# Transposes of the softmax weights moved from a step's middle to the next step's beginning, in a hybrid decoder layer

## The chip, the cores and the metric

The kernel runs on one core of a Trainium2 chip. The metric is the device time of one execution in microseconds (us). The engines are TensorE (PE; PEld is its weight load), VectorE (DVE), ScalarE (ACT), GpSimd (POOL) and SyncE (SP), which issues most DMAs. Each engine works through its own list of instructions in the order in which the program wrote them; semaphores tie the lists together.

## The reference

One decoder layer over 512 positions, width 2048, in float32. Cut to what matters:

```python
h = rmsnorm(x, g_pre_attn) * (1 + sc_a) + sh_a          # sc_a, sh_a: adaLN, silu(c) @ w_ada
qa, ka, va, qb, kb, vb = split(h @ w_in)                 # 8 heads A, 8 heads B, 128 wide
qa, ka, qb, kb = rope(...)
oa = rmsnorm(dilated_mixture_attention(qa, ka, va), g_out_a)     # group A: three dilated windows
s = einsum('bqmhe,bkmhe->bmhqk', qb, kb); a = softmax(causal(s)) # group B: two maps a head
ob = rmsnorm(einsum('bhqk,bkhe->bqhe', a[:,0] - lam * a[:,1], vb), g_subln) * (1 - lambda_init)
x = x + gt_a * rmsnorm(concat([oa, ob]) @ w_out, g_post_attn)
h = rmsnorm(x, g_pre_ffn) * (1 + sc_f) + sh_f
x = x + gt_f * rmsnorm((silu(h @ w_gate) * (h @ w_up)) @ w_down, g_post_ffn)
```

## The kernel before

The program is a list of 610 steps. Each step takes one weight tile of 128x1024 and multiplies it: steps 0 to 79 are the input projections, 80 to 143 the output projection (64 shorter steps), 144 onward the feed-forward part. Float32 accuracy comes from three products for each: a weight tile is split into a high part (w_hi, a ScalarE copy, L1710) and the rest (w_lo, a VectorE subtraction, L1719), and both meet the split activations. A step of the projections has 24 such products of 512 columns (L277 to L279, or L282 to L284), in two halves of 12. The split for step i + 2 is made during step i.

All other work is hung onto the steps by lists of functions. The loop over steps runs them in this order, and that sets every engine's order:

```
start_ev, pe_ev (by a number: 0, 1, 2), start2_ev, first half of the products, w_hi for i+2,
mid_ev, mid_act, second half of the products, post_ev, post_late + rope1, w_lo for i+2, rope2, dots, post_end
```

Attention runs in steps 20 to 79, beside the projections, as 56 units. A unit is one block of 128 queries of one head (for the first two blocks of a head of group A: both at once). A head of B has four units, a head of A three, and a planner places at most one unit in a step, in the order of the heads. A unit has these stages:

- s0, at a step's beginning: the scores on TensorE (L507 for B, L500 for A) into bank 4 or 5, on VectorE the mask with the row maximum (L512) and its negative (L515), on ScalarE the exponential (L516) into misc_p.
- s0b (post_late, B alone): VectorE joins the two maps (L521 to L524).
- s1, in the middle of the next step: one to four transposes of 128x128 on TensorE (L529) into bank 6. s1b: the ScalarE copy of them out of bank 6 (L534), into misc_pt, or into pts for the heads A4 to A7.
- s2, at the beginning of the step after: the products with V (L545) into bank 7. The heads A4 to A7 do theirs in steps 81 to 84.

After the last unit of a head its output is normalised: a, the ScalarE copy out of bank 7 (L558); b, four squares with row sums on ScalarE (L568), for B behind a VectorE maximum (L563 to L566); c, VectorE's small operations on the sums (L575 to L584) and a power on GpSimd (L585); c2, one step later, the scaling on VectorE (L589, L590); d, four transposes of the result (L595) into bank 6 as well, with the ScalarE copy L597 out of it.

In the same steps run the rotations of queries and keys: the evacuation of a finished projection (L413) and DMAs that swap rows, issued by ScalarE (L399), and one or two steps later three VectorE operations of 1024 columns (L426 to L428).

What fills the rest of VectorE are the dots: 96 products with row sums over tiles of w_ada (L228), for the adaLN values that are needed later. Each takes a tile of its own, loaded by SyncE (L1695) through the same four buffers as the weight tiles. The planner walks through the steps, adds up what TensorE, VectorE and the loads have to do (pe_cost, dve_cost and constants), and gives each step none, one or two dots, and each rotation its step, so that VectorE's sum stays near the end of TensorE's sum. Moving a cost from one step to another therefore shifts dots and rotations too. One group of 16 values is turned into a row by a transpose (L1018, with the copy L1020), two steps after its last dot, in the middle of a step and in bank 6.

In the output projection (steps 80 to 143) VectorE also splits the attention's result (L843) and scales finished sums (L1146).

Of the kernel before, what the change touches and what calls it, by code (L numbers as in the profile page):

```python
# [34 lines left out]
def body(tc, t):  # L35
# [5 lines left out]
    with ctx:  # L41
# [273 lines left out]
        pe_ev = defaultdict(list)  # L315
        mid_ev = defaultdict(list)
        post_ev = defaultdict(list)
# [284 lines left out]
        pe_cost = defaultdict(float)  # L602
        dve_cost = defaultdict(float)

        def place_unit(n, kind, head, qbs, hn, s):
            s0, s0b, s1, s1b, s2 = unit_stages(n, kind, head, qbs)
            m = 1 if kind == "A" else 2
            for qb in qbs:
                N = 128 * (qb + 1)
                pe_cost[s] += m * max(0.218, 0.00168 * N)  # L610
                dve_cost[s] += m * (0.4 + N / 960) + (1.0 + 1.6 * N / 960 if kind == "B" else 0)
                pe_cost[s + 1] += 0.107 * (qb + 1)
            if 0 in qbs:
                def mk(kind=kind, head=head):
                    h = HST[kind, head]
                    hs = sp.tile([128, 5, 4], F, name="hst", tag="hst", bufs=4)
                    for i, k in enumerate(("den", "ss", "f", "rd", "nb")):
                        h[k] = hs[:, i, :]
                pe_ev[s].append((0, mk))
            pe_ev[s].append((2, s0))  # L620
            post_late[s].append(s0b)
            mid_ev[s + 1].append(s1)
            mid_act[s + 1].append(s1b)
            if kind == "A" and head >= 4:
                late_pv[head].append(s2)
                assert s + 1 < W0
                return
            for qb in qbs:
                pe_cost[s + 2] += 0.218 * (qb + 1)
            pe_ev[s + 2].append((0, s2))  # L630
            if 3 in qbs:
                a, b, c, c2, d = head_post(kind, head, hn)
                start2_ev[s + 2].append(a)
                mid_act[s + 2].append(b)
                post_late[s + 2].append(c)
                post_ev[s + 3].append(c2)
                pe_ev[s + 4].append((1, d))
                dve_cost[s + 2] += 1.0 if kind == "A" else 1.6
                dve_cost[s + 3] += 0.8
                pe_cost[s + 4] += 0.43  # L640

        late_pv = defaultdict(list)

# [11 lines left out]
        post_late = defaultdict(list)  # L655
        rope1, rope2 = defaultdict(list), defaultdict(list)
        mid_act = defaultdict(list)
        dve_late = defaultdict(float)
        post_end = defaultdict(list)
        start2_ev = defaultdict(list)  # L660
# [204 lines left out]
        W0 = NPROJ  # L865
# [3 lines left out]
        for jj, kp in enumerate(KP_ORDER):  # L869
            for k in range(2):  # L870
                kc = 2 * kp + k
                s = wsteps[0, 0, jj, 0]
# [177 lines left out]
        for h in range(4, 8):  # L1050
            s = W0 + 1 + (h - 4)
# [4 lines left out]
        for i in range(W0 + 60):  # L1056
            mm_t = 5.13 if i < W0 else 2.57
            if todo:
                hn, k, h, qbs = todo[0]
                if need[k, h] == 0 and avail.get((k, h), -1) < i:  # L1060
                    todo.pop(0)
                    place_unit(nu, k, h, qbs, hn, i)
                    nu += 1
                    if not todo:
                        scored = i
# [199 lines left out]
        def act_tr(g, half, src, banks):  # L1265
            st = {}

            def go_pe():
                a = v3(src(), 2)
                for f in range(2):  # L1270
                    st[f] = ps = PS(banks[f], (128, 2, 256))
                    for n in range(2):
                        for tl_ in range(2):
                            c = 128 * (2 * n + f)
                            pe.transpose(ps[:, n, 128 * tl_:128 * tl_ + 128], a[:, tl_, c:c + 128], ident)  # L1275

            def go_v():
                stage.add(src())
                p = actv[g, f"v{half}"] = stage.get()
                for f in range(2):  # L1280
                    act.activation(v3(p, 4)[:, 2 * f:2 * f + 2, :], st[f], AF.Copy)
            return go_pe, go_v
# [105 lines left out]
        for hf, at in ((0, F0 + 32), (1, F0 + 36)):  # L1388
            a, b = act_tr(0, hf, lambda hf=hf: ffn["f0", hf], (6, 7))
# [10 lines left out]
        for g in range(1, 11):  # L1400
# [13 lines left out]
            a, b = act_tr(g, 0, lambda g=g: ffn[g, "s1"], (6, 7))  # L1414
            pe_ev[b0 + 27].append((0, a))
            post_ev[b0 + 27].append(b)
            a, b = act_tr(g, 1, lambda g=g: ffn[g, "c21"], (6, 7))
# [156 lines left out]
        for i in range(8):  # L1574
            a, b = h2_tr(0, i, 4 + i % 4)
# [16 lines left out]
        for i in range(8):  # L1592
            a, b = h2_tr(1, i, 4 + i % 4)
# [183 lines left out]
        for i in range(NSTEP):  # L1777
# [10 lines left out]
            s = steps[i]  # L1788
# [148 lines left out]
```

## Time and profile before

| | us |
|---|---|
| median of 3 runs (lowest, highest) | 2186.57 (2186.1, 2186.99) |
| the profiled execution | 2187.89 |
| its span, first to last instruction | 2186.1 |
| steps 20 to 79, from first to last | about 230 to 676 |

The profile shows one execution. Busy times of engines overlap. A row of time order reads: start, length, engine, line, operation, what it writes and reads, and in brackets the idle time of the engine before it and what ended that. A row of the waits reads: who waited for whom, total us, times, longest. A row of a group of instructions ends with its busy time and mean ns, and the idle time before them.

### The profile page before, as it was taken

What the parts mean: (1) busy time and instruction counts of PE and PEld (TensorE: products, weight loads), DVE (VectorE), ACT (ScalarE), POOL (GpSimd) and SP (SyncE); (2) the same over time, 40 slices, a digit from 0 to 9 for tenths busy, and PEclk for the clock granted to TensorE, in tenths of its full rate; (3) what the DMA queues carried; (4) which work ended last, traced back from release to release, by engine and by line L of the source; (5) the groups of instructions that cost most, each with busy time, mean ns of one, the idle gap of its engine ahead of it and who ended that gap; (6) DMA issues with size and microseconds to landing.
All of it is one profiled execution on the core that took longest, in us unless ns stands there. A gap on an engine that the chain in (4) does not pass through costs nothing.

```text
span 2186.1 us, 26913 instructions
## 1 busy us (share of the span) xinstructions
PE 2152.3 (98%) x9748; PEld 1758.3 (80%) x9748; DVE 1671.9 (76%) x2337; ACT 1058.1 (48%) x1541; POOL 103.7 (5%) x112
## 2 busy tenths in 40 slices
PE   7999999999999999999999999999999999999998
PEld 6888777778888788787888888888888888888886
DVE  6987877776777775896777777677777788898877
ACT  5443344444435565654545555554554553444443
POOL 0000000001001000000001001000000000000000
PEclk8999999999999999999999999999999999999999
DMA  9797634555678877787779769778777889999986
GB/s 374 298 347 227 170 113 155 168 157 173 208 239 275 285 248 262 264 291 220 219 228 271 224 207 289 214 202 267 241 223 221 279 310 410 381 386 369 345 304 264
DMA packets 160452, 564.39 MB, mean 258 GB/s; under 512 B 17440, under 2 KB 17728, under 8 KB 153920
## 3 DMA queue, kind: packets, MB, share of 16 engines
q1 hardware_dynamic: 142608, 502.09, 64.0%
q0 software_dynamic: 10944, 39.85, 10.2%
q10 hardware_dynamic: 6768, 20.73, 3.1%
q8 instruction: 77, 1.26, 0.2%
q14 instruction: 55, 0.45, 0.1%
HBM read 499.67 MB, written 54.02 MB: 253 GB/s over the span
## 4 chain that ended last, share of the span: by engine, by line
PE 88%; DMA 5%; DVE 4%; ACT 1%; issue 1%; SPq 0%; ACTq 0%; POOL 0%; DVEq 0%
PE b L283 22%; PE b L282 22%; PE b L284 22%; PE b L277 6%; PE b L279 5%; PE b L278 5%; PE b L507 2%; DMA w_raw<-in_wout 2%; DVE w_lo L1719 1%; DMA a<-acts 1%; PE b L545 1%; PE b L1275 1%; PE b L500 1%; PE b L529 1%; ACT w_hi L1710 1%
## 5 line engine op out<-in xcount | busy, mean ns | idle before, releaser
L1719 DVE TENSOR_TENSOR w_lo<-raw,w_hi 128x1024 fp32r<-128x1024 f32 x236 | 286.8, 1221 | 155.2 <-ACT w_hi L1710 155.1
L1710 ACT ACTIVATE w_hi<-raw 128x1024 fp32r<-128x1024 f32 x236 | 249.5, 1061 | 291.1 <-PE b L284 219.8
L282 PE MATMUL b<-w_hi,h 128*128 128x512 f32 x864 | 342.9, 397 | 0.4 <-ACT xT L212 0.4
L283 PE MATMUL b<-w_lo,h 128*128 128x512 f32 x864 | 337.0, 390 | 0.8 <-DVE w_lo L1719 0.7
L284 PE MATMUL b<-w_hi,h 128*128 128x512 f32 x864 | 336.9, 390 | 0.0
L1719 DVE TENSOR_TENSOR w_lo<-w_raw,w_hi 128x1024 fp32r<-128x1024 f32 x176 | 214.0, 1221 | 60.7 <-ACT w_hi L1710 60.5
L1710 ACT ACTIVATE w_hi<-w_raw 128x1024 fp32r<-128x1024 f32 x176 | 185.6, 1056 | 152.1 <-PE b L284 66.1
L282 PE MATMUL b<-w_hi,e 128*128 128x512 f32 x640 | 250.3, 391 | 4.1 <-ACT w_hi L1710 4.1
L283 PE MATMUL b<-w_lo,e 128*128 128x512 f32 x640 | 250.8, 392 | 1.0 <-DVE w_lo L1719 1.0
L284 PE MATMUL b<-w_hi,e 128*128 128x512 f32 x640 | 250.0, 391 | 0.0
L283 PE MATMUL b<-w_lo,a 128*128 128x512 f32 x616 | 240.0, 390 | 1.3 <-DVE w_lo L1719 1.3
L282 PE MATMUL b<-w_hi,a 128*128 128x512 f32 x616 | 240.0, 390 | 0.7 <-DMA a<-acts 0.7
L284 PE MATMUL b<-w_hi,a 128*128 128x512 f32 x616 | 239.7, 389 | 0.0
L1710 ACT ACTIVATE w_hi<-w_lent 128x1024 fp32r<-128x1024 f32 x130 | 137.8, 1061 | 172.8 <-PE b L284 130.3
L277 PE MATMUL b<-h,w_hi 128*128 128x512 f32 x512 | 213.4, 417 | 0.0
L278 PE MATMUL b<-h,w_hi 128*128 128x512 f32 x512 | 201.1, 393 | 1.4 <-DVE h L273 1.4
L279 PE MATMUL b<-h,w_lo 128*128 128x512 f32 x512 | 201.5, 394 | 0.0
L1719 DVE TENSOR_TENSOR w_lo<-w_lent,w_hi 128x1024 fp32r<-128x1024 f32 x130 | 158.5, 1220 | 56.0 <-ACT w_hi L1710 55.7
L282 PEld LDWEIGHTS b<-w_hi,h 128*128 128x128 f32 x864 | 162.3, 188 | 37.0 <-issue 3.8
L283 PEld LDWEIGHTS b<-w_lo,h 128*128 128x128 f32 x864 | 162.4, 188 | 35.3 <-DVE w_lo L1719 2.3
L284 PEld LDWEIGHTS b<-w_hi,h 128*128 128x128 f32 x864 | 162.2, 188 | 34.1
L516 ACT ACTIVATE misc_p<-misc_p,stt 128x128 f32<-128x128 f32 (+3 forms) x96 | 54.0, 562 | 190.2 <-DVE stt L515 171.5
(358 smaller groups left out, 3504.2 us busy)
## 6 DMA issues: line engine op xcount, KB each, us to landing
a<-acts SPq DMA_DIRECT2D x154, 512.0 KB, 5.7
raw<-in_wgu SPq DMA_DIRECT2D x131, 512.0 KB, 6.0
w_raw<-in_win SPq DMA_DIRECT2D x107, 512.0 KB, 4.9
w_raw<-in_adar SPq DMA_DIRECT2D x96, 512.0 KB, 4.6
w_lent<-in_wgu SPq DMA_DIRECT2D x69, 512.0 KB, 6.8
w_raw<-in_wout SPq DMA_DIRECT2D x64, 512.0 KB, 4.9
acts<-stage SPq DMA_DIRECT2D x49, 512.0 KB, 4.2
raw<-in_wds SPq DMA_DIRECT2D x48, 512.0 KB, 6.4
```

The source lines that it names most:

```text
L277: pe.matmul(ps, whi, ahi, start=start, stop=False, **kw)
L278: pe.matmul(ps, whi, alo, start=False, stop=False, **kw)
L279: pe.matmul(ps, wlo, ahi, start=False, stop=stop, **kw)
L282: pe.matmul(ps, ahi, whi, start=start, stop=False, **kw)
L283: pe.matmul(ps, ahi, wlo, start=False, stop=False, **kw)
L284: pe.matmul(ps, alo, whi, start=False, stop=stop, **kw)
L500: pe.matmul(sc[:, r], qk[:, i, qs], qk[:, i + 1, :N], start=True, stop=True)
L507: pe.matmul(sc[:, :N], qk[k, 2 * m, qs], qk[k, 2 * m + 1, :N], start=True, stop=True)
L516: act.activation(p, p, AF.Exp, bias=nm, scale=scale, accum_out=den)
L529: pe.transpose(tr[:, j, :], misc["p"][:, n % 2, 128 * j:128 * j + 128], ident)
L1710: act.activation(hi, raw, AF.Copy)
L1719: dve.tensor_tensor(lo, raw, hi.bitcast(F), op=OP.subtract)
```

## The change

Six entries of the function that places a unit change:

- s1 and s1b go from the middle of step s + 1 to step s + 2: the transposes to its beginning, behind the products with V of the unit before and ahead of the new scores; the copy behind the exponentials of that step and ahead of the weight split.
- s2 goes from step s + 2 to step s + 3, and a, b, c, c2 one step later with it.
- d goes from the beginning of step s + 4 to the middle of step s + 5.
- The planner's costs move to the same steps.

```diff
@@ place_unit
-                pe_cost[s + 1] += 0.107 * (qb + 1)
+                pe_cost[s + 2] += 0.107 * (qb + 1)
...
             pe_ev[s].append((2, s0))
             post_late[s].append(s0b)
-            mid_ev[s + 1].append(s1)
-            mid_act[s + 1].append(s1b)
+            pe_ev[s + 2].append((1, s1))
+            start2_ev[s + 2].append(s1b)
             if kind == "A" and head >= 4:
                 late_pv[head].append(s2)
-                assert s + 1 < W0
+                assert s + 2 < W0
                 return
             for qb in qbs:
-                pe_cost[s + 2] += 0.218 * (qb + 1)
-            pe_ev[s + 2].append((0, s2))
+                pe_cost[s + 3] += 0.218 * (qb + 1)
+            pe_ev[s + 3].append((0, s2))
             if 3 in qbs:
                 a, b, c, c2, d = head_post(kind, head, hn)
-                start2_ev[s + 2].append(a)
-                mid_act[s + 2].append(b)
-                post_late[s + 2].append(c)
-                post_ev[s + 3].append(c2)
-                pe_ev[s + 4].append((1, d))
-                dve_cost[s + 2] += 1.0 if kind == "A" else 1.6
-                dve_cost[s + 3] += 0.8
-                pe_cost[s + 4] += 0.43
+                start2_ev[s + 3].insert(0, a)
+                mid_act[s + 3].append(b)
+                post_late[s + 3].append(c)
+                post_ev[s + 4].append(c2)
+                mid_ev[s + 5].append(d)
+                dve_cost[s + 3] += 1.0 if kind == "A" else 1.6
+                dve_cost[s + 4] += 0.8
+                pe_cost[s + 5] += 0.43
```

The units keep their steps. The order of the instructions changes at these places, among others.

TensorE, step 64 before: the beginning of the step where the head A2 ends its work. First the end of step 63, then the step's own work, up to its first product; bank 7 is b_4450, bank 6 is b_4511.

```order
L279 MATMUL b_4283<-h_3_220,w_lo 128x512
L545 MATMUL b_4450<-VA_3018,misc_pt 128x128 [waits Activation_49]
L545 MATMUL b_4450<-VA_3018,misc_pt 128x128 x2
L595 MATMUL b_4511<-cst,misc_pt 128x128 [waits DVE_49,PE_49]
L595 MATMUL b_4511<-cst,misc_pt 128x128 x3
L500 MATMUL b_4518<-A_4267 128x128
L500 MATMUL b_4518<-A_4267 128x256
L277 MATMUL b_4527<-h_0_442,w_hi 128x512
```

TensorE, step 65 of the change, where the same head's L595 now stand: the last products of the first half, the transposes, the first products of the second half. Their bank 6 (b_4570) was written at this step's beginning by L529 (as b_4544).

```order
L277 MATMUL b_4501<-h_1_606,w_hi 128x512
L278 MATMUL b_4501<-h_1_616,w_hi 128x512
L279 MATMUL b_4501<-h_1_606,w_lo 128x512
L595 MATMUL b_4570<-cst,misc_pt 128x128 [waits DVE_49,Activation_49]
L595 MATMUL b_4570<-cst,misc_pt 128x128 x3
L277 MATMUL b_4502<-h_1_606,w_hi 128x512
L278 MATMUL b_4502<-h_1_616,w_hi 128x512
```

The transposes went from the beginning to the middle, and wait for ScalarE in place of an earlier instruction of TensorE.

ScalarE, steps 65 and 66 before (from the exponential of step 65), and then the same two steps of the change:

```order
L516 ACTIVATE misc_p,hst<-misc_p,stt 128x384 [waits DVE_49]
L558 ACTIVATE misc_pt<-b_4450 128x512 [waits PE_49]
L1710 ACTIVATE w_hi<-w_raw 128x1024 [waits DMAHW6_49]
L568 ACTIVATE junk,hst<-misc_pt 128x128 [waits Activation_49] x4
L534 ACTIVATE pts_4604<-b_4596 128x384 [waits PE_49]
L516 ACTIVATE misc_p,hst<-misc_p,stt 128x512 [waits DVE_49]
```

```order
L516 ACTIVATE misc_p,hst<-misc_p,stt 128x384 [waits DVE_49,PE_49]
L534 ACTIVATE misc_pt<-b_4544 128x512 [waits PE_49]
L1710 ACTIVATE w_hi<-w_raw 128x1024 [waits DMAHW1_49]
L597 ACTIVATE mixT_4212<-b_4570,cst 128x512 [waits PE_49]
L516 ACTIVATE misc_p,hst<-misc_p,stt 128x512 [waits DVE_49,PE_49,Activation_49]
L558 ACTIVATE misc_pt<-b_4481 128x512
L534 ACTIVATE pts_4613<-b_4602 128x384
```

The copy L534 went from the step's end to right behind the exponential, ahead of the weight split L1710 (and, where a head ends, ahead of the squares L568, which follow that split); L558 comes a step later, and L597 stands in the middle.

VectorE, steps 96 to 99 of the change in the output projection:

```order
L843 TENSOR_TENSOR mixlo_5798<-mixT_2288,mixhi_5797 128x256 x2
L1719 TENSOR_TENSOR w_lo<-w_raw,w_hi 128x1024
L228 SCALAR_TENSOR_TENSOR w_raw,red<-w_raw,p_82 128x1024
L1146 TENSOR_TENSOR u_5791<-b_5307,gtg_5203 128x512
L1146 TENSOR_TENSOR u_5793<-b_5314,gtg_5203 128x512
L1719 TENSOR_TENSOR w_lo<-w_raw,w_hi 128x1024
L228 SCALAR_TENSOR_TENSOR w_raw,red<-w_raw,silu_b 128x1024
L843 TENSOR_TENSOR mixlo_5798<-mixT_2288,mixhi_5797 128x256 x2
L1146 TENSOR_TENSOR u_5791<-b_5346,gtg_5203 128x512
L1146 TENSOR_TENSOR u_5793<-b_5357,gtg_5203 128x512
L1719 TENSOR_TENSOR w_lo<-w_raw,w_hi 128x1024 x2
L228 SCALAR_TENSOR_TENSOR w_raw,red<-w_raw,p_82 128x1024
```

Before, no L228 stood there: the last one was in step 94. Four dots more than before lie behind step 80: in steps 96, 97, 99 and 100, each with its load. Among the projections' steps some dots change places, the rotations of the heads B6, B7, A0 and A1 stand one step earlier (steps 29, 33, 45 and 49), and the row transpose L1018 goes from the middle of step 49 to the middle of step 54.

## The prediction

> **What bounds the kernel now.** I read the page's first part and its chain of waits, then the table of waits of TensorE, then the busy time by stretches, and last the engines in order of time around the attention work.
>
> ```profile
> PE 2152.3 (98%) x9748; PEld 1758.3 (80%) x9748; DVE 1671.9 (76%) x2337; ACT 1058.1 (48%) x1541; POOL 103.7 (5%) x112
> PE 88%; DMA 5%; DVE 4%; ACT 1%; issue 1%; SPq 0%; ACTq 0%; POOL 0%; DVEq 0%
> ...
> PE b L283 <- DVE w_lo L1719: 4.8, 9, 0.7
> PE b L529 <- ACT tabs L1020: 0.4, 1, 0.4
> ...
> 313.80:482.00 168.20, 167.84 (x771) 128.23 (x770) 129.12 (x343) 76.60 (x189) 5.03 (x5) 1.00 0.49 151
> 482.00:571.80 89.80, 89.80 (x454) 73.53 (x453) 62.28 (x134) 40.78 (x101) 7.39 (x4) 1.00 0.60 194
> 579.50:675.80 96.30, 96.30 (x441) 77.46 (x440) 68.19 (x128) 37.84 (x78) 1.82 (x1) 1.00 0.75 237
> 727.60:736.70 9.10, 8.47 (x37) 6.63 (x36) 6.24 (x10) 3.18 (x3) 0.00 (x0) 1.00 0.94 321
> 736.70:745.90 9.20, 8.49 (x38) 6.73 (x37) 8.26 (x12) 7.55 (x16) 0.00 (x0) 1.00 0.77 233
> 745.90:764.00 18.10, 18.10 (x81) 14.83 (x80) 10.62 (x15) 9.57 (x15) 0.00 (x0) 1.00 0.84 300
> ```
>
> In a stretch the first number is its length, the next the busy time of TensorE, then weight loads, VectorE, ScalarE. While the moved work runs (steps 20 to 79, about 230 to 676 us) TensorE never stops but for 0.4 us, the one wait of L529. So nothing there can be won by ending a wait; the change wins only if its transposes take fewer TensorE slots, and loses if it makes TensorE wait. TensorE does stop in the output projection, steps 80 to 97.
>
> **The transposes themselves: 0.** A step's products are issued 0.23 us apart.
>
> ```profile
> 303.07 0.39 PE L279 MATMUL b<-h,w_lo 128*128 128x512 f32 x1
> 303.30 0.27 PE L529 MATMUL b<-cst,misc_p 128*128 128x128 f32 x1
> 303.33 0.48 PE L277 MATMUL b<-h,w_hi 128*128 128x512 f32 x1
> 303.64 0.39 PE L278 MATMUL b<-h,w_hi 128*128 128x512 f32 x1
> ...
> 314.25 0.60 PE L595 MATMUL b<-cst,misc_pt 128*128 128x128 f32 x4
> 314.78 1.98 PE L507 MATMUL b<-B 64*128 64x512 f32 x4
> ```
>
> One transpose in the middle moves L278 from 303.30 + 0.23 = 303.53 to 303.64: 0.11 us. Four of the same form at a step's beginning take 314.78 - 314.25 = 0.53, 0.13 each. With 160 transposes the move costs at most 160 x 0.02 = 3 us. Of 56 middles with transposes 12 keep some (the heads' L595 go there) and 44 are freed; if each saves the lag of the product behind it (0.48 - 0.39 = 0.09) that is a gain of 4 us. The 0.11 already holds this lag, so I take 0, with -4 and +3 as ends.
>
> **The new wait: L595 in the middle of a step.** Before, bank 6 was written by L529 in the middle and by L595 at a beginning, so the ScalarE copy L534 had half a step to empty it. Now in each of the 12 steps that hold L595 the same step's L529 has filled bank 6 at its beginning, and L595 waits for L534. On ScalarE that copy stands behind the step's exponentials (L516), which wait for VectorE's masks (L512). Behind L595 on TensorE stand the 12 products of the second half: they wait too, and TensorE has nothing else. How late are the exponentials?
>
> ```profile
> 556.98 1.05 PE L545 MATMUL b<-VA,misc_pt 128*128 128x128 f32 x8
> 561.29 0.49 PE L529 MATMUL b<-cst,misc_p 128*128 128x128 f32 x3
> 565.04 1.02 PE L500 MATMUL b<-A 128*128 128x512 f32 x2
> ...
> 560.33 0.58 ACT L558 ACTIVATE misc_pt<-b 128x512 f32<-128x512 f32 x1
> 560.81 1.05 ACT L1710 ACTIVATE w_hi<-w_raw 128x1024 fp32r<-128x1024 f32 x1
> 561.76 0.30 ACT L568 ACTIVATE junk<-misc_pt 128x128 f32<-128x128 f32 x1
> 563.36 0.47 ACT L534 ACTIVATE misc_pt<-b 128x384 f32<-128x384 f32 x1
> ...
> 563.48 0.16 DVE L576 TENSOR_TENSOR hst<-hst 128x4 f32<-128x4 f32 x1 [3.77 <-ACT junk L568]
> 563.96 1.22 DVE L1719 TENSOR_TENSOR w_lo<-w_raw,w_hi 128x1024 fp32r<-128x1024 f32 x1
> 565.09 1.22 DVE L228 SCALAR_TENSOR_TENSOR w_raw<-w_raw,silu_b 128x1024 f32<-128x1024 f32 x1
> 567.39 0.68 DVE L512 CUSTOM_DVE_ANT_0 misc_p<-b,tabs 128x512 f32<-128x512 f32 x1
> ```
>
> This is step 62 before, where a head ends. Its exponential ends at 560.33. Then ScalarE copies the head (0.48), splits weights (0.95) and squares (to 563.36); VectorE stands 3.77 us in L576 until the squares are there, then splits (to 565.09) and does two dots (to 567.39): 7.06 us in all. So the next step's mask starts at 567.39 although its scores were issued at 565.04. Nobody on TensorE minds that today. After the change L534 stands ahead of the weight split and of the squares: 0.47 more, 7.5.
>
> Group A in the new order, in us from each step's start: in the step where a head ends the exponential ends at 4.1 (products with V, transposes and scores 2.1, 0.4 to the mask, 0.9 mask, 0.7 exponential), VectorE is free at 11.6. That step lasts 7.6 (step 63's 7.4, and two more L545 of 0.12), so this is 4.0 into the next one. There two masks and exponentials take 1.6, then copy 0.5, weight split 0.95, VectorE's split 1.15, two dots 2.3: 10.5, and as this step lasts 7.1 it is 3.4 into the third, the one with L595. Mask and exponential (1.4) and a copy of four tiles (0.58) end at 5.4. TensorE comes to L595 at 4.5: 561.29 - 556.98 = 4.31 before, less two L545, more four L529. **Wait 0.9 us.** The rows that change it:
>
> ```profile
> 581.98 1.23 DVE L228 SCALAR_TENSOR_TENSOR w_raw<-w_raw,p 128x1024 f32<-128x1024 f32 x1 [3.25 <-DMA w_raw<-in_adar]
> 583.13 0.55 DVE L512 CUSTOM_DVE_ANT_0 misc_p<-b,tabs 128x384 f32<-128x384 f32 x1
> 584.53 0.58 ACT L558 ACTIVATE misc_pt<-b 128x512 f32<-128x512 f32 x1
> ```
>
> Step 56 follows a B head, whose squares take longer, and the row transpose of L1018: 1.5. Step 59: the step where its head ends (57) has a rotation and no dots: 0. Step 62: no dots in step 61, but the rotation (3 x 1.2) in their place: 0.9. Step 65: the second dot of step 64 waited for its load until 581.98, 10.2 into that step, while the rotation's row swaps were under way. That load is issued once an earlier dot ends, now up to 2.3 later; I take half of it: dot over at 12.6, 5.5 into step 65, copy over at 7.5, wait 3.0 (0.9 if the load is not later, 5 if by all of it). Step 68: step 67 is 0.7 shorter and L595 comes at 3.8: 4.1 + 1.4 + 0.6 - 3.8 = 2.3. Sum of group A **+7.7**, ends 1 and 13.
>
> Group B:
>
> ```profile
> 289.70 0.47 ACT L534 ACTIVATE misc_pt<-b 128x384 f32<-128x384 f32 x1
> ...
> 291.74 2.45 ACTq L399 DMA_DIRECT2D p<-B  x4
> ...
> 295.02 1.05 ACT L1710 ACTIVATE w_hi<-w_raw 128x1024 fp32r<-128x1024 f32 x1
> ...
> 295.19 0.60 PE L529 MATMUL b<-cst,misc_p 128*128 128x128 f32 x4
> ```
>
> In step 28 (and 32) ScalarE issues four swaps for 2.45 us ahead of the exponentials, which end at 295.02; a copy of 0.47 then ends at 295.5, the middle comes at about 295.2: 0.35 each. In steps 40 and 44 VectorE has one dot in each of the two steps before; the same count gives a wait between 0.1 and 0.7, I take 0.4. The other four have their copy over before the middle. **+1.5**, ends 0 and 4. The 0.4 of L529 behind L1020 goes; L1018 itself, now in the middle of step 54, waits for a copy about as long: 0, within 0.5 either way.
>
> **The dots that move: +2.2.** The planner's step ends shift, and four dots (L228) with their loads go from the projections, where they cost TensorE nothing, to steps 96, 97, 99 and 100. Steps 90 to 97 have such dots already, five loads in three steps through four buffers: each three steps last 9.1 to 9.2 us, with 0.63 and 0.71 of it idle, where the stretch behind has no idle. Two more rounds: 1.3 at least.
>
> ```profile
> 744.82 2.35 DVE L1719 TENSOR_TENSOR w_lo<-w_raw,w_hi 128x1024 fp32r<-128x1024 f32 x2
> ...
> 745.86 0.39 PE L282 MATMUL b<-w_hi,mixhi 128*128 128x512 f32 x1
> ```
>
> VectorE has no room there: of its two splits the one that step 100 (from 745.86) needs ends about 746.0. Two dots of 1.2 ahead of it put it 2.4 later, less some waits that they fill: 2.2, at most 4.
>
> **Sum.** 0 + 7.7 + 1.5 + 0 + 2.2 = +11.4. The profiled execution took 2187.89 us (span 2186.1 and 1.8 around it), so 2199.3 by it; it stands 1.3 over the runs' median of 2186.57, hence **2198.0** for the runs. A comparison of this kernel can tell about 0.2%, 4.4 us, from no change.
>
> **Rivals.**
>
> *Not slower: VectorE catches up.* The mechanism is the same chain, in the third step: if the mask there starts 1 us earlier than I count (dots landing in time, handoffs shorter by some 0.1 each over ten links), the copy is over before TensorE reaches L595, and only steps 28 and 32 and the two rounds of dots are left: 0.7 + 1.3 = 2, that is 2188.6. For it speaks VectorE's busy time, 62 of 90 us in group A; against it that it stands in L576 for 3.77 us in order while the later work queues.
>
> *Faster: the freed middles.* All 44 save 0.09 and no copy is late: 2186.6 - 4.0 = 2182.6. It needs the wait of L595 never to bind.
>
> *The clock drops.* The trace has a long stop of TensorE at 1005.7:
>
> ```profile
> 1005.70:1009.90 4.20, 0.10 (x1) 0.10 (x1) 0.12 (x1) 3.25 (x5) 0.00 (x0) 1.00 0.77 152
> 1009.90:1016.70 6.80, 6.21 (x14) 4.56 (x15) 5.65 (x6) 2.87 (x4) 0.00 (x0) 0.50 0.73 235
> ```
>
> After 4.1 us idle the granted clock (third from the right) is 0.50 for 6.8 us, which loses 3.4. A stop of over 3 but not 4 us may or may not do this; step 65's, at its upper end of 5, would: 11.4 + 2.0 + 3.4 = +16.8, 2203.4. [...]
>
> *All of VectorE's lateness adds up.* Every new wait at its upper end: 3 + 13 + 4 + 0.5 + 4 = 24, less what one late step spares the next; I take +20, 2206.6.
>
> **How the numbers follow.** The forecast 0.53, VectorE catches up 0.23, freed middles 0.03, clock 0.10, all adds up 0.11. The forecast's own range is 2192 to 2203. The range from 2187.5 to 2206 takes in the first rival and the clock, and leaves out the gain and the worst. Slower by over 0.2% (over 2190.9) are the forecast but a sliver, the clock and the worst: 0.72. Within 0.2%: 0.25. Faster: 0.03.
>
> **What would show it.** In the waits of TensorE a new row L595 behind ACT L534 (misc_pt or pts), about ten times, some 9 us, longest at step 65 and near 3; L529 in no row. TensorE idle in the stretch from 482 to 676, none before. L283 behind VectorE at steps 100 and 103 where it now stops at 97. If L595 has no row, the chain of masks was counted too long, and the forecast fails there; if the steps' lengths change without idle time, the price of a transpose is wrong; if the output projection shows no new idle, the dots were free.

## The result, and the profile after

The changed kernel takes 2198.48 us (median of 4 runs, 2196.63 to 2199.55) and the kernel before 2186.78 (4 runs, 2186.10 to 2187.36). The ratio is 1.0049, 95% interval 1.0036 to 1.0061: slower, by 11.7 us. The profiled execution took 2199.29 us with a span of 2197.5, against 2187.89 and 2186.1.

The page's share of TensorE and its chain, changed kernel:

```profile
PE 2154.6 (98%) x9748; PEld 1760.1 (80%) x9748; DVE 1673.9 (76%) x2337; ACT 1053.7 (48%) x1541; POOL 103.7 (5%) x112
...
PE 82%; DVE 8%; DMA 6%; ACT 3%; issue 1%; SPq 0%; ACTq 0%; POOL 0%; DVEq 0%
```

TensorE has the same 9748 matmuls and 2.3 us more busy time, while the span grew by 11.4. In the chain its share fell from 88% to 82%; VectorE's rose from 4% to 8%, ScalarE's from 1% to 3%. The waits of TensorE in the changed kernel (total us, times, longest):

```profile
PE b L283 <- DVE w_lo L1719: 7.5, 10, 2.1
...
PE b L595 <- ACT misc_pt L534: 3.0, 5, 1.3
PE b L282 <- DMA a<-acts: 2.1, 2, 1.8
PE b L595 <- ACT pts L534: 2.0, 1, 2.0
PE b L595 <- DVE misc_p L590: 1.5, 1, 1.5
```

The new wait is there: L595 behind the copy L534, six times, 5.0 us, where the prediction named about ten and some 9 us; the longest is in step 68, not in step 65. L529 is in no row any more. L283 behind the splits grew from 4.8 to 7.5. Where the time went, by the stretches of steps 20 to 51, 52 to 79 and 80 to 111, of the kernel before and of the changed one (length, then busy time of TensorE, weight loads, VectorE, ScalarE, GpSimd, granted clock, DMA share, GB/s):

```profile
229.77:482.01 252.24, 251.87 (x1148) 192.44 (x1148) 194.80 (x507) 111.88 (x278) 7.06 (x7) 1.00 0.50 150
482.01:675.85 193.84, 193.84 (x936) 157.58 (x934) 135.63 (x274) 82.39 (x187) 9.21 (x5) 1.00 0.69 216
675.85:778.65 102.80, 99.29 (x482) 82.10 (x480) 74.28 (x122) 55.16 (x107) 7.28 (x4) 1.00 0.81 270
```

```profile
229.80:479.39 249.59, 249.08 (x1137) 191.09 (x1137) 190.59 (x494) 107.78 (x275) 7.06 (x7) 1.00 0.47 142
479.39:679.23 199.84, 195.28 (x947) 159.04 (x946) 135.88 (x278) 81.72 (x190) 9.21 (x5) 1.00 0.66 213
679.23:787.38 108.15, 100.97 (x481) 81.92 (x480) 79.77 (x131) 55.37 (x108) 7.29 (x4) 1.00 0.80 274
```

Steps 20 to 51 became 2.65 shorter, steps 52 to 79 6.0 longer (4.56 of it idle, none before), steps 80 to 111 5.35 longer. The three make +8.7 of the 11.4. Another 3.0 lies in steps 144 to 175, where nothing was changed (92.79 us before, 95.80 after); the part on the prediction comes back to it.

The longest of the new waits, in step 68: TensorE in order of time, then ScalarE.

```profile
604.72 0.39 PE L279 MATMUL b<-h,w_lo 128*128 128x512 f32 x1
607.13 0.66 PE L595 MATMUL b<-cst,misc_pt 128*128 128x128 f32 x4 [2.02 <-ACT pts L534]
607.54 0.48 PE L277 MATMUL b<-h,w_hi 128*128 128x512 f32 x1
```

```profile
602.57 1.12 ACTq L399 DMA_DIRECT2D p<-A  x2
605.88 0.61 ACT L516 ACTIVATE misc_p<-misc_p,stt 128x384 f32<-128x384 f32 x1 [3.34 <-DVE stt L515]
606.41 0.19 ACT L516 ACTIVATION_READ_ACCUMULATOR misc_p<-misc_p,stt 128x1 f32 x1
606.50 0.57 ACT L534 ACTIVATE pts<-b 128x512 f32<-128x512 f32 x1
```

ScalarE stands 3.34 us in its exponential, which waits for VectorE's mask, and only then makes the copy that TensorE waits for. The tiles of that copy had been in bank 6 since the step's beginning. The mask itself (L512) starts as soon as VectorE has ended the second of two dots (L228):

```profile
603.89 1.22 DVE L228 SCALAR_TENSOR_TENSOR w_raw<-w_raw,p 128x1024 f32<-128x1024 f32 x1
605.04 0.55 DVE L512 CUSTOM_DVE_ANT_0 misc_p<-b,tabs 128x384 f32<-128x384 f32 x1
```

### The profile page after: what moved, and what is told of

Its sections match the earlier page's. It is cut to its first block, busy times and chain, and to the rows that moved or that the text cites. A ratio compares the mean times of both kernels' runs of the same rounds, so it can differ in the third digit from the quotient of the medians.

```text
span 2197.5 us, 26940 instructions
## 1 busy us (share of the span) xinstructions
PE 2154.6 (98%) x9748; PEld 1760.1 (80%) x9748; DVE 1673.9 (76%) x2337; ACT 1053.7 (48%) x1541; POOL 103.7 (5%) x112
## 4 chain that ended last, share of the span: by engine, by line
PE 82%; DVE 8%; DMA 6%; ACT 3%; issue 1%; SPq 0%; ACTq 0%; POOL 0%; DVEq 0%
PE b L283 21%; PE b L282 21%; PE b L284 21%; PE b L277 4%; PE b L278 4%; PE b L279 4%; DVE w_lo L1719 2%; DMA w_raw<-in_wout 2%; PE b L507 2%; DMA a<-acts 1%; DVE w_raw L228 1%; ACT w_hi L1710 1%; PE b L545 1%; PE b L1275 1%; ACT misc_p L516 1%
## 5 line engine op out<-in xcount | busy, mean ns | idle before, releaser
L1719 DVE TENSOR_TENSOR w_lo<-raw,w_hi 128x1024 fp32r<-128x1024 f32 x236 | 286.9, 1221 | 159.0 <-ACT w_hi L1710 158.9
L1710 ACT ACTIVATE w_hi<-raw 128x1024 fp32r<-128x1024 f32 x236 | 249.4, 1060 | 296.8 <-PE b L284 223.8
L282 PE MATMUL b<-w_hi,h 128*128 128x512 f32 x864 | 342.6, 397 | 0.4 <-ACT xT L212 0.4
L283 PE MATMUL b<-w_lo,h 128*128 128x512 f32 x864 | 337.8, 391 | 2.2 <-DVE w_lo L1719 2.1
L1719 DVE TENSOR_TENSOR w_lo<-w_raw,w_hi 128x1024 fp32r<-128x1024 f32 x176 | 214.2, 1221 | 73.9 <-ACT w_hi L1710 73.6
L1710 ACT ACTIVATE w_hi<-w_raw 128x1024 fp32r<-128x1024 f32 x176 | 185.7, 1057 | 153.6 <-PE b L284 58.8
L282 PE MATMUL b<-w_hi,e 128*128 128x512 f32 x640 | 250.3, 391 | 3.2 <-ACT w_hi L1710 3.2
L283 PE MATMUL b<-w_lo,e 128*128 128x512 f32 x640 | 250.7, 392 | 0.9 <-DVE w_lo L1719 0.5
L282 PE MATMUL b<-w_hi,a 128*128 128x512 f32 x616 | 240.1, 390 | 2.1 <-DMA a<-acts 2.1
L283 PE MATMUL b<-w_lo,a 128*128 128x512 f32 x616 | 240.1, 390 | 0.8 <-DVE w_lo L1719 0.8
L1710 ACT ACTIVATE w_hi<-w_lent 128x1024 fp32r<-128x1024 f32 x130 | 138.0, 1061 | 169.3 <-PE b L284 128.6
L1719 DVE TENSOR_TENSOR w_lo<-w_lent,w_hi 128x1024 fp32r<-128x1024 f32 x130 | 158.6, 1221 | 50.8 <-ACT w_hi L1710 50.5
L282 PEld LDWEIGHTS b<-w_hi,h 128*128 128x128 f32 x864 | 162.7, 188 | 37.2 <-issue 3.7
L283 PEld LDWEIGHTS b<-w_lo,h 128*128 128x128 f32 x864 | 162.7, 188 | 37.0 <-DVE w_lo L1719 3.9
```

Source lines behind the costliest of these rows:

```text
L282: pe.matmul(ps, ahi, whi, start=start, stop=False, **kw)
L283: pe.matmul(ps, ahi, wlo, start=False, stop=False, **kw)
L1710: act.activation(hi, raw, AF.Copy)
L1719: dve.tensor_tensor(lo, raw, hi.bitcast(F), op=OP.subtract)
```

## The experiments

The experiments in a table first, with stretches in us from the traces (steps 20 to 79 are the attention, 80 to 111 the first half of the output projection). Times of runs are to be read by the ratio to the kernel before on the same chip.

| kernel | median | ratio, 95% interval | steps 20–79 | 80–111 |
|---|---|---|---|---|
| before | 2186.78 | 1 | 446.1 | 102.8 |
| changed | 2198.48 | 1.0049 (1.0036, 1.0061) | 449.4 | 108.2 |
| 1 copy first | 2189.36 | 1.0009 (1.0001, 1.0018) | 443.1 | 108.4 |
| 2 old planner costs | 2196.67 | 1.0041 (1.0027, 1.0055) | 455.4 | 101.3 |
| 3 both | 2183.62 | 0.9983 (0.9974, 0.9991) | 443.1 | 100.0 |
| 4 before, new planner costs | 2196.65 | 1.0040 (1.0027, 1.0052) | 448.3 | 109.6 |
| 5 other bank | 2185.73 | 0.9989 (0.9980, 0.9998) | 445.0 | 102.5 |
| 6 both, dots early | 2183.81 | 0.9983 (0.9974, 0.9992) | 443.1 | 97.9 |
| 7 before, dots early | 2196.07 | 1.0036 (1.0024, 1.0049) | 455.8 | 98.0 |
| 8 both, half of that | 2186.01 | 0.9995 (0.9986, 1.0004) | 446.0 | 98.7 |
| 9 both, dots early from step 16 | 2184.52 | 0.9982 (0.9973, 0.9990) | 446.2 | 97.9 |
| 10 L595 at the beginning | 2214.46 | 1.0121 (1.0107, 1.0135) | 469.9 | 103.7 |
| 11 before, dots early from step 16 | 2192.53 | 1.0023 (1.0014, 1.0032) | 457.0 | 97.9 |
| 12 as 9, row transpose later | 2180.41 | 0.9963 (0.9949, 0.9976) | 443.1 | 98.0 |

### 1. The copy ahead of the exponentials

The changed kernel, but the copy L534 is issued right behind its transposes, ahead of the step's exponentials.

```diff
             pe_ev[s + 2].append((1, s1))
-            start2_ev[s + 2].append(s1b)
+            pe_ev[s + 2].append((1.5, s1b))
```

> The change, but the ScalarE copy of the transposes (L534) is issued right behind the transposes and ahead of the step's exponentials; everything else, the dots too, as in the change. Theory (L595 waits in the middle because L534 stands behind the exponentials): the six rows of L595 behind L534 (4.9 us of idle, some 5.5 with the slow restart) vanish, the output projection keeps its loss: about 2193, 5.5 under the change. Rival (VectorE is what is late, the copy only shows it): L595 or another line waits as long for VectorE, 2197 to 2199.

Measured: 2189.36 us, 9 us below the changed kernel and 3.6 below what was expected. No row of L595 behind L534 is left. Step 68 on ScalarE, in order of time:

```profile
598.88 0.60 ACT L534 ACTIVATE pts<-b 128x512 f32<-128x512 f32 x1 [1.20 <-PE b L500]
600.73 0.62 ACT L516 ACTIVATE misc_p<-misc_p,stt 128x384 f32<-128x384 f32 x1 [1.25 <-DVE stt L515]
```

The copy now fills time in which ScalarE waits for the mask. Steps 20 to 79 take 443.1 us, 3.0 less than before the change: without the wait the change is a gain there. Against the changed kernel this stretch won 6.3 us. Another 2.3 of the difference lie in steps 144 to 175 (93.5 us here, 95.8 there), which the edit does not touch. Steps 80 to 111 stay at 108.4, so that part of the loss has nothing to do with bank 6.

### 2. The planner's costs where they were

The changed kernel, but with the five cost lines as before, so that dots and rotations stand in their old steps.

```diff
-                pe_cost[s + 2] += 0.107 * (qb + 1)
+                pe_cost[s + 1] += 0.107 * (qb + 1)
...
-                dve_cost[s + 3] += 1.0 if kind == "A" else 1.6
-                dve_cost[s + 4] += 0.8
-                pe_cost[s + 5] += 0.43
+                dve_cost[s + 2] += 1.0 if kind == "A" else 1.6
+                dve_cost[s + 3] += 0.8
+                pe_cost[s + 4] += 0.43
```

> The change, but the planner's costs stay on the steps of the kernel before, so that dots and rotations stand where they stood before. Theory: steps 80 to 112 last 102.8 us again in place of 108.2 (the four moved dots are all of that loss), L595 still waits 4 to 6 us in the middles: about 2193. Rival (the loss in the output projection comes from heads A4 to A7 arriving later or from SyncE's loads, not from the dots): 107 to 108 there, 2198.

Measured: 2196.67, more than expected. The four moved dots are back and steps 80 to 111 take 101.3 us, but the waits in the attention have grown:

```profile
PE b L595 <- ACT misc_pt L534: 6.7, 9, 1.7
...
PE b L595 <- ACT pts L534: 2.0, 1, 2.0
```

Ten waits and 8.7 us, against six and 5.0. Steps 40 and 44, which had none in the changed kernel, wait 0.93 and 0.95 here; in the step ahead of each stand two dots where the changed planner puts one. A dot more on VectorE, 1.22 us each, is here a mask later, an exponential later, a copy later. Of the 6.0 us by which steps 20 to 79 grew over the changed kernel, 3.7 are such waits and 1.7 is a drop of the clock behind the one in step 68 (last section). So the two parts of the change are not additive: the planner's shift cost time in the output projection and saved some in the attention.

### 3. Both

Edits 1 and 2 together: the moved transposes alone, with the copy ahead.

> The change with both: L534 ahead of the exponentials, and the planner's costs on the old steps. Theory: both losses gone, what is left is what the freed middles save, 2.7 us in steps 20 to 52 and as much again at most behind: 2183 to 2185, under the kernel before. Rival (freed middles save nothing, steps 20 to 52 were shorter by chance): 2187.

Measured: 2183.62, ratio 0.9983 with the interval below 1: slightly faster than before, as the theory had it. TensorE does not stop from step 20 to 79:

```profile
229.77:478.61 248.84, 248.84 (x1137) 191.31 (x1137) 194.53 (x506) 112.25 (x276) 7.06 (x7) 1.00 0.49 153
478.61:672.85 194.24, 194.24 (x946) 159.32 (x945) 136.88 (x275) 84.89 (x190) 9.22 (x5) 1.00 0.67 217
```

### 4. The planner's costs alone

The kernel before with the moved cost lines, the transposes left in the middle.

> The kernel before with nothing but the planner's costs moved as in the change: its dots and rotations, the old places of all attention work. Theory: no L595 wait in a projection step, steps 20 to 80 within 0.5 us of before, steps 80 to 112 at 107 to 108 us: about 2192. Rival (dots cost only beside the moved attention work): 2187.

Measured: 2196.65, worse than the theory's figure by 4.7 us. Steps 80 to 111 take 109.6 us, close to the 108.2 and 108.4 of the other two kernels with 19 dots behind step 80, so the dots cost by themselves (1.7 of the 109.6 is 3.4 us at half clock). Steps 20 to 79 grew by 2.2, most of it a wait of TensorE that had been priced at nothing:

```profile
PE b L529 <- ACT tabs L1020: 1.8, 1, 1.8
```

The row transpose L1018 falls into step 54 by the new costs, where with L529 in the middle it is again two uses of bank 6 at one place.

### 5. Another bank

Kernel 2, the copy still behind the exponentials; ten of the twelve L595 write into one of the projections' banks that is free then, in place of bank 6.

```diff
-                tr = PS(head if last else 6, (128, 4, 128))
+                tr = PS(head if last else h["bank"], (128, 4, 128))
...
+                HST[kind, head]["bank"] = {28: 0, 40: 2, 44: 0, 48: 2, 52: 0, 56: 2,
+                                           59: 2, 62: 0, 65: 2, 68: 0}.get(s + 5, 6)
```

> The change with the planner's costs where they stood before the change (so dots and rotations stand in their old steps, +9.9 us measured), and with the copy L534 still behind the exponentials; only the ten L595 that share a bank with the same step's L529 and waited for L534 (8.7 us of waits in the same kernel without this edit) go to a bank that is free then. Theory (the shared bank 6 is the cause): the row L595 behind ACT L534 falls from ten waits and 8.7 us to at most two (steps 32 and 36 keep bank 6) and under 1 us, steps 20 to 79 take about 437 us instead of 455, no: as much less than the 455.4 measured as the waits and their restarts made, 8.7 + 10 x 0.2 = 11, so 444 to 445, and the time comes to 2196.7 - 11 = 2186, within 2184 to 2189. Rival (VectorE is late in these steps whatever the bank, and TensorE stops anyway, at L545 or L529 for misc_pt or the weights at L283): the idle time stays and moves to other rows, time 2193 to 2197.

Measured: 2185.73, 0.9989 of the kernel before where kernel 2 had 1.0041: 11 us less, as expected. The one wait behind L534 that is left is that of step 32, which kept bank 6:

```profile
PE b L595 <- ACT misc_pt L534: 1.5, 1, 1.5
```

The order on ScalarE and VectorE is that of kernel 2, and the copy stands as late in it. So the shared bank is the cause, and the late copy the price of sharing it. The wait of step 32 is longer than in kernel 2 (0.46), since ScalarE took 3.77 us to issue the four row swaps ahead of the exponentials, 2.70 there:

```profile
321.61 3.77 ACTq L399 DMA_DIRECT2D p<-B  x4
325.43 0.40 ACT L516 ACTIVATE misc_p<-misc_p,stt 128x128 f32<-128x128 f32 x1 [3.85 <-issue]
```

### 6 and 8. Fewer dots behind step 80

Kernel 3 with the planner's margin for dots raised, which puts them into earlier steps: 1.0 us leaves none behind step 80, 0.6 us seven (15 before, 19 in the changed kernel).

```diff
-M_ADA = -0.05
+M_ADA = 1.0
```

> The change with the planner's costs as before, the copy L534 ahead of the exponentials (2183.62 measured with both), and the planner's margin for dots raised from -0.05 to 1.0 us, by which all dots fit into the projections and none is left behind step 80. Theory (the stops of the output projection's beginning come from the dots' rounds on VectorE): L283 behind VectorE has no row in steps 80 to 97, steps 80 to 111 take about 98 us instead of 99.97, and steps 20 to 79 stay at 443.1 within 1: 2181 to 2182.5. Rival (VectorE is then late in the projections: masks and splits come behind the added dots): steps 20 to 79 grow by 2 to 6 us with rows of L545 or L529 or L282/L283 behind VectorE and ScalarE, and the time is 2184 to 2188.

> As the kernel with all dots early, but with a margin of 0.6 us, by which about seven dots stay behind step 80. Theory (each round of dots behind step 80 costs about 0.6): between the kernel with the old margin (2183.62) and the one with all dots early, steps 80 to 111 at 98.5 to 99.5, 2182 to 2183.5. Rival (VectorE late in the projections): steps 20 to 79 longer by 1 to 3 us than 443.1, 2184 to 2186.

Measured: 2183.81 and 2186.01, both above what the theory said. Steps 80 to 111 did as it said or better. With no dots (kernel 6), with seven (8), with 15 (3) and with 19 (1), a row each, lengths first:

```profile
678.24:776.17 97.93, 97.93 (x481) 82.57 (x480) 55.62 (x86) 55.55 (x107) 4.85 (x4) 1.00 0.58 190
```

```profile
676.61:775.32 98.71, 98.12 (x481) 82.52 (x480) 65.22 (x106) 55.24 (x107) 7.29 (x4) 1.00 0.72 236
```

```profile
672.85:772.83 99.98, 98.89 (x482) 82.26 (x481) 73.98 (x122) 55.00 (x107) 7.28 (x4) 1.00 0.82 275
```

```profile
672.78:781.13 108.35, 101.98 (x482) 83.08 (x480) 79.27 (x130) 55.15 (x107) 7.28 (x4) 0.98 0.80 274
```

The loss over 97.9 is 0, 0.8, 2.1 and 10.4; of the 10.4, 1.7 is 3.4 us at half clock (the 0.98 in the last row). With 15 dots it was 4.9 in the kernel before and 3.3 and 4.5 in kernels 2 and 5, so this stretch varies by some 3 us at the same order. The first 18 of its steps (80 to 97) vary so: 59.9 us without dots, 61.9 to 65.2 with 15 or 19. The steps behind them tell the last four dots apart: steps 98 to 111 take 38.1 to 38.7 us in every kernel with at most 15 dots, and 43.0, 45.5 and 47.1 in those with 19 (changed, 1, 4; the last two with 1.7 from the clock). The last four dots thus cost 4.3 to 7.2 us, and the 15 ahead of them 2.0 to 5.3 in all.

What was gained there was lost elsewhere. In kernel 6 four dots moved into the first steps, and step 16 stopped for VectorE:

```profile
213.37 1.05 PE L736 MATMUL b<-junk,p 128*128 128x1 f32 x8 [3.20 <-DVE VB L668]
```

Steps 16 to 19 took 28.7 us in place of 23.6: the stop, and 3.4 us at half clock after it. VectorE came late to L668 because the dot ahead of it had stood 2.56 us for its load. This profiled execution was the slowest of kernel 6's eleven (2187.94, median 2183.81), and with the same four dots there the stop was 1.7 us in kernel 7 and 0.7 in kernel 8, so a usual run of kernel 6 may have lost less than these 5.1 us. In kernel 8 the row transpose fell into step 44, and L595 waited 2.19 us for its copy L1020: steps 20 to 79 grew by 2.9, as the rival had it, though mostly for the bank and not for late masks (0.36 behind L534 in step 28).

### 7 and 11. The same margin in the kernel before

The kernel before with the margin of 1.0 us, from step 0 on (7) and from step 16 on (11).

> The kernel before, with nothing but the planner's margin for dots raised from -0.05 to 1.0 us. Theory (each of the two effects is its own: dots cost where they stand, the transposes' places something else): steps 80 to 111 fall from 102.8 to about 98-100, steps 20 to 79 stay at 446 or grow by up to 2 because the transposes in the middle wait for later exponentials: 2183 to 2186. Rival (the transposes at the beginning are what makes room for early dots): steps 20 to 79 grow by 5 or more with L529 behind VectorE's or ScalarE's work, time 2189 to 2194.

> The kernel before with the dots' margin raised to 1.0 us from step 16 on only. Theory (with the transposes in the middle a fuller VectorE costs TensorE in steps 20 to 51 what it did with the margin from step 0, 8 us, most of it one wait of L529 behind L1020 with the lower clock after it): steps 20 to 79 at 449 to 456, steps 80 to 111 at 98, L545 behind L534 several times; median 2187 to 2194, over the changed kernel with the same margin by 6 to 12. Rival (the loss came from the row transpose's wait alone, which falls differently here): steps 20 to 79 at 446 to 448, median 2181 to 2185.

Measured: 2196.07 and 2192.53. For kernel 7 the theory fell: steps 20 to 79 grew by 9.8 (its rival had 5 or more), and the time is over the rival's 2194 too. But 3.0 of the 9.8 is L529 behind the row transpose's copy L1020, with 6.8 us at half clock after it, and only 2.8 are waits for L534. For kernel 11 the theory's time held, with steps 20 to 79 at 457.0, 1.0 over its range; the largest wait is not the one that it named, L529 behind L1020 (0.4 here), but L545 behind L534. Kernel 11's steps 20 to 51, its waits, and ScalarE ahead of the longest:

```profile
229.74:491.39 261.65, 256.70 (x1149) 193.85 (x1149) 203.43 (x522) 111.61 (x278) 7.06 (x7) 0.99 0.50 161
...
PE b L545 <- ACT misc_pt L534: 5.8, 8, 3.0
...
237.95 5.75 ACTq L399 DMA_DIRECT2D swp<-B  x3
245.69 0.26 ACT L534 ACTIVATE misc_pt<-b 128x128 f32<-128x128 f32 x1
```

With the transposes in the middle the copy L534 stands at a step's end, and the products with V at the next beginning wait for it when ScalarE comes late: by 0.24 to 0.28 us six times and 1.23 once with the fuller VectorE, and by 3.0 in step 22, where ScalarE issued row swaps for 5.75 us ahead of the exponentials and the copy. That one wait, with 6.8 us at half clock behind it, is 6.4 of the 10.9 us by which steps 20 to 79 grew; the swaps began 2.3 us later than in the kernel before, and whether the dots made them late was not tried apart. With the transposes at the beginning and the copy ahead (kernels 6, 9 and 12) L545 never waits for L534 with such dots, though the same swaps took 7.19 us in kernel 9 and 6.39 in kernel 12. So the change does make room for a late ScalarE and a fuller VectorE, if the copy goes first.

### 9 and 12. The best of it

Kernel 3 with the margin of 1.0 us from step 16 on (two dots behind step 80), and then with the row transpose one step later.

```diff
-            ... t_end + (M_ADA if i < W0 else M_ADAW) ...
+            ... t_end + ((1.0 if i >= 16 else M_ADA) if i < W0 else M_ADAW) ...
```

> The change with the planner's costs as before and the copy L534 ahead of the exponentials (2183.62 measured), and the dots' margin raised to 1.0 us from step 16 on only: two dots are left behind step 80 (15 without it). The kernel with that margin from step 0 lost 5.1 us in steps 16 to 19, where L736 waited 3.2 us for VectorE's VB L668 and the granted clock then fell, and won 2.0 us in steps 80 to 111. Theory (both effects are local to their place): steps 16 to 19 back at 23.6, steps 20 to 79 at 443.1, steps 80 to 111 at 98: profiled span 2179 to 2183, median 2179 to 2182. Rival (the dots left out of the first steps make VectorE late in steps 20 to 79): these grow by 2 to 6 us, median 2183 to 2187.

Measured: 2184.52, above the theory's 2179 to 2182. Steps 16 to 19 were back at 23.6 and steps 80 to 111 at 97.9, but steps 20 to 51 took 251.9: again the row transpose in step 44, in the same middle and the same bank as L595 (2.19 us), and a wait of 0.54 for L534 in step 28.

```diff
-                    mid_ev[i + 2].insert(0, row[1])
+                    mid_ev[i + 3].insert(0, row[1])
```

> The changed kernel with the copy L534 ahead of the exponentials, the planner's costs as before the change and the dots' margin of 1.0 us from step 16 on (2184.52 measured, 2182.7 of span), and the row transpose L1018 with its copy L1020 one step later. In step 44 it stood in the same middle and the same bank as L595, which waited 2.2 us for L1020. Theory (one more case of two uses of bank 6 at one place): that wait goes with its restart of 0.2, steps 20 to 51 fall from 251.92 to about 249.5, and the median to 2181.5 to 2182.5. Rival (L595 then waits at step 44 for the copy L534 or for VectorE's L590, or L529 for L1020 in step 46): steps 20 to 51 stay over 251, median 2184 to 2185.

Measured: 2180.41 (2179.82 to 2182.71), ratio 0.9963, interval 0.9949 to 0.9976. It is the fastest of all, some 18 us under the changed kernel and 1.1 under the theory's range. TensorE does not stop from step 20 to 111:

```profile
229.96:478.80 248.84, 248.84 (x1137) 191.32 (x1137) 203.25 (x522) 111.90 (x276) 7.07 (x7) 1.00 0.53 169
478.80:673.04 194.24, 194.24 (x946) 159.33 (x945) 142.60 (x287) 84.58 (x190) 9.21 (x5) 1.00 0.71 231
673.04:770.99 97.95, 97.95 (x482) 82.57 (x481) 59.13 (x94) 55.40 (x107) 5.67 (x4) 1.00 0.61 211
```

### 10. The heads' transposes back at the beginning

Kernel 2 with L595 and its copy L597 at the beginning of the step, ahead of L529.

```diff
-                mid_ev[s + 5].append(d)
+                pe_ev[s + 5].append((1, d))
```

> The change with the planner's costs as before (2196.67 measured), but with the heads' transposes L595 and their copy L597 at the beginning of the step, ahead of L529, in place of the middle; the copy L534 stays behind the exponentials. Theory (two uses of bank 6 a step need one ScalarE copy between them, wherever the second one stands): no row of L595 behind L534, but a new row of L529 behind L597 in up to 12 steps, 0.7 to 1.5 us each, 8 to 16 us in all, and a median of 2195 to 2203. Rival (only the place behind the exponentials is what costs; a copy at a step's beginning finds ScalarE free): L529 waits 0.1 to 0.4 each, 1 to 4 us in all, median 2187 to 2190.

Measured: 2214.46, worse than either had it; the theory held in kind and was too low in size.

```profile
PE b L529 <- ACT mixT L597: 20.6, 12, 3.3
```

All twelve steps wait, up to 3.34 us in step 32, where ScalarE still issues the row swaps of the step before:

```profile
326.48 2.69 ACTq L399 DMA_DIRECT2D p<-B  x4
329.21 0.69 ACT L597 ACTIVATE mixT<-b,g_sub 128x512 f32<-128x512 f32 x1 [2.76 <-issue]
```

The middle was the better place of the two. Steps 20 to 79 are 14.5 us longer than in kernel 2: the longer waits make 11.9 (20.6 against 8.7) and the 6.8 us more at half clock 3.4, a little over the whole. Another 2.4 lie in steps 80 to 111.

## Why the prediction was right, point by point

The time was forecast at 2198.0 and is 2198.48, and the mechanism is the one described. That the two figures lie so close is luck: the errors of the terms cancel. By its terms, on the profiled executions:

| term | forecast | measured |
|---|---|---|
| the transposes themselves | 0 (−4 to +3) | −2.5 |
| L595 behind L534, group A | +7.7 | +5.3 (4.5 idle, the rest restart, 0.2 for each of four) |
| the same, group B | +1.5 | +0.9 (0.5 idle, two restarts) |
| row transpose and L529's wait | 0 | −0.3 |
| the four dots (steps 80 to 111) | +2.2 (up to 4) | +5.35, 4.8 of it in steps 98 to 111 |
| everything behind step 111 | 0 | +2.7 |
| sum | +11.4 | +11.4 (parts rounded) |

**The bank.** That the wait would be L595's, behind a copy behind exponentials behind masks, is shown by kernels 1 and 5, which take away the copy's late place and the shared bank, each alone: kernel 1 ends every such wait, and kernel 5 ends it in all the steps whose L595 left bank 6. By step the forecast was 1.5, 0, 0.9, 3.0 and 2.3 for steps 56, 59, 62, 65 and 68; measured 1.35, none, 0.52, 0.65 and 2.02. Steps 28 and 32: 0.35 each, measured 0.20 and 0.31. Steps 40 and 44: 0.4 each, none measured.

**Step 65 is the mis-sized one: 3.0 against 0.65.** The forecast let the second dot of step 64 wait for its load, and took half of a further lateness. VectorE of the changed kernel there:

```profile
579.50 1.22 DVE L228 SCALAR_TENSOR_TENSOR w_raw<-w_raw,p 128x1024 f32<-128x1024 f32 x1
580.65 0.08 DVE L228 DVE_READ_ACCUMULATOR w_raw<-w_raw,p 128x1 f32 x1
580.65 1.22 DVE L228 SCALAR_TENSOR_TENSOR w_raw<-w_raw,silu_b 128x1024 f32<-128x1024 f32 x1
```

The second dot follows the first without a gap: its load was issued at 574.26, later than before (572.50), but landed in 6.1 us and not in 9.5. The row swaps that ran beside it were over at 577.9, where before they ran to 584.7. The forecast carried the lateness of one execution over to a step in which the transfers met differently; its own alternative for a load in time, 0.9, was close.

**The transposes themselves: −2.5, in the bounds but not nothing.** Kernel 3 shows it undisturbed: steps 20 to 79 take 443.1 us against 446.1, of which 0.5 is L529's wait. A round of four steps of group B takes 31.57 us against 31.73, and one of three of group A 22.41 against 22.49. In a freed middle the second half of a step takes 2.72 us where it took 2.84 (the forecast had 0.09 of lag for this), and the longer beginnings take about half of it back.

**The dots: 5.35 against 2.2.** The step that failed took two rounds at the price of the rounds already there, and let L1719 be late by at most two dots. Steps 98 to 111, where the four dots work, took 43.0 us against 38.2, so 4.8 of the 5.35 and over the upper end of 4; some 0.6 lies in steps 80 to 90, where L595 waited 0.65 in step 86 in place of 0.15. In the changed kernel VectorE works from 745.6 to 754.5 without a gap, the splits that TensorE waits for behind a dot and two sums:

```profile
747.96 1.22 DVE L228 SCALAR_TENSOR_TENSOR w_raw<-w_raw,silu_b 128x1024 f32<-128x1024 f32 x1
749.10 0.09 DVE L228 DVE_READ_ACCUMULATOR w_raw<-w_raw,silu_b 128x1 f32 x1
749.10 0.76 DVE L843 TENSOR_TENSOR mixlo<-mixT,mixhi 128x256 fp32r<-128x256 f32 x2
749.84 1.29 DVE L1146 TENSOR_TENSOR u<-b,gtg 128x512 f32<-128x512 f32 x2
751.04 2.35 DVE L1719 TENSOR_TENSOR w_lo<-w_raw,w_hi 128x1024 fp32r<-128x1024 f32 x2
```

L283 waits at steps 99 (0.60), 100 (1.20) and 105 (0.76), where the forecast named 100 and 103, and at 105 L282 waits 0.76 for a weight split on ScalarE, which the forecast had not: that split waited for the load of its weights. (The dots' loads go through the same four buffers; whether it was they that made this one late was not tried apart.) That the dots are the cause is shown by kernel 4: it moves the planner's costs alone, by which only these dots differ behind step 80, and takes 109.6 us there. Kernel 2 moves them back alone and takes 101.3.

**Behind step 111** the forecast had nothing. The 3.0 us of steps 144 to 175 are a wait at step 163, L283 behind L1719, which is 1.4 longer (2.09 us here, 0.70 before, and between 0.47 and 2.06 in the kernels of the experiments, with no order to it), and 1.7 for 3.4 us at half clock after it. Why that wait varies was not tried, so 2.7 of the measured 11.4 stay without a cause that the change explains.

**The rivals.** VectorE did not catch up, save in steps 40 and 44, and its lateness did not add up to 20 us either. The freed middles save, but the copies were late. The clock did drop in the profiled execution, but behind the stop of step 163 (2.09 us idle, then 3.41 us at 0.50) and not in step 65, where TensorE waited 0.65 us. The forecast's sum leaves the clock at 1.00 behind a stop of 3.0 us; no run shows that, and in kernels 6, 7 and 11 half clock followed stops of 3.20, 3.0 and 3.0 us.

## What to carry to other kernels

Two pieces of work shared bank 6, and ScalarE, which had to empty it, stood 3.34 us in an exponential ahead of the copy (step 68 of the changed kernel): when work is moved, look what the emptying engine has ahead of its copy, and put the copy ahead of whatever waits. Here that one place was worth 6.3 us of the attention's 449.4 with the moved costs (changed kernel, 1) and 12.4 with the old ones (2, 3; 1.7 of it the clock's), and another bank won 10.4 of these 12.4. A planner's cost lines are part of the change: moved with the work they shifted filler to a place where it cost 5 us, so run the move with the old plan too. And where VectorE had no room left, the last four dots cost about as much as the 15 before them, or more (4.3 to 7.2 us against 2.0 to 5.3): read the price of filler from the place where it lands, not from the average of what is already there.

## What the runs showed of the hardware

The forecast added nothing for the clock to its stop of 3.0 us in step 65. In step 68 of kernel 2 half clock followed a stop of 2.03 us. Two stretches of that kernel, then two of the changed kernel around its stop in the same step, and two around its step 163 (third number from the right: granted clock):

```profile
609.21:612.63 3.42, 1.39 (x9) 0.92 (x8) 1.35 (x5) 1.94 (x4) 0.00 (x0) 1.00 0.98 274
612.63:616.04 3.41, 3.41 (x9) 2.64 (x8) 3.18 (x4) 0.77 (x2) 0.00 (x0) 0.50 1.00 340
```

```profile
603.37:606.78 3.41, 1.74 (x8) 1.12 (x6) 2.38 (x7) 0.90 (x3) 0.00 (x0) 1.00 0.91 233
606.78:610.20 3.42, 3.07 (x16) 2.61 (x17) 2.15 (x2) 1.82 (x3) 0.00 (x0) 1.00 1.01 313
...
934.44:937.85 3.41, 1.32 (x6) 0.79 (x5) 3.41 (x5) 2.00 (x2) 0.00 (x0) 1.00 0.01 4
937.85:941.26 3.41, 3.41 (x10) 2.66 (x9) 3.38 (x7) 0.00 (x0) 0.00 (x0) 0.50 0.81 298
```

In kernel 2 TensorE was idle for 2.03 of the 3.42 us, and the next 3.41 us ran at 0.50, which cost 1.7 us more. In step 163 of the changed kernel it was idle for 2.09 us, and again 3.41 us at 0.50 followed. In step 68 of the changed kernel the stop was 2.02 us, and the clock stayed at 1.00. So of three stops of 2.0 to 2.1 us two cost 1.7 us more, and one nothing more; what makes the difference was not shown. Half clock also followed longer stops: 3.20 us in kernel 6 (3.4 us at half clock) and 3.0 us in each of kernels 7 and 11 (6.8 us each).
